# Transformer encoder block on one Trainium2 core: the down projection by seven products of halves

## Chip, core and metric

The kernel runs on one core of one Trainium2 chip. TensorE multiplies matrices, VectorE, ScalarE and GpSimd do the elementwise work, SyncE issues transfers. The metric is the device time of one execution in microseconds (us), lower is better.

## What is computed

One encoder layer over 512 positions and 1024 channels, in float32: two parallel token mixers (multi-scale pooling, and a gated delta rule in both directions), their merge, and a gated feed-forward part. The change concerns the feed-forward part alone:

```python
h2 = rmsnorm(x, norm2_w[l])
u = dwconv_centered(h2 @ ffn_up[l], ffn_conv_w[l], ffn_conv_b[l])   # 1024 -> 2 x 2816, width 3
gate, val = jnp.split(u, 2, axis=-1)
x = x + (jax.nn.silu(gate) * val) @ ffn_down[l]                     # 2816 -> 1024
return rmsnorm(x, final_norm_w)
```

## The kernel before

Every large product runs in float32 quality as three matmuls in a reduced-precision float32 format: each operand is split into a high part (rounded, a ScalarE copy) and a low part (the rest, a subtraction), and `mm3` adds high x high, high x low and low x high into one PSUM bank.

**Order.** The kernel first declares all its work as tasks (`A` for ScalarE, `V` VectorE, `G` GpSimd, `M` TensorE, `L` a transfer issued by SyncE), each with the tiles it reads and writes, an estimated cost and a key. `Planner.run` plays these tasks through with the costs, takes on each engine the ready task with the lowest key, and honours rings of buffers (`RINGS`: name and number of buffers). The instructions are then issued in the order found. Each engine works strictly in that order, so an instruction that waits holds up all that stand behind it on its engine, and a transfer that waits on SyncE holds up all later transfers.

**Up projection.** For each of 22 channel blocks c there are two units, gate and value. A unit loads a weight block of 1024x128 (ring `raw`, 3 buffers), ScalarE casts it to the high part (`whi`, 2 buffers), GpSimd makes the low part in two subtractions of 128x512 (`wlo`, 2 buffers), and TensorE does 24 matmuls with 512 positions as columns into a PSUM bank (`pp`, 3 banks). ScalarE and VectorE turn the bank into the convolution (`conv3`, ring `cv3`, 4 buffers of 128x512). After both units: SiLU on ScalarE, product on VectorE, then the split of the product into high (ScalarE) and low part (VectorE), kept as `a_hl[c]` for the down projection.

**Down projection.** Two halves of the output channels (`hf`). In each, for 22 blocks of 128 rows of `ffn_down` (two per load, split as above by `weights`) and four token tiles of 128 (`t`), three matmuls of 128x128 by 128x512, accumulated over the 22 blocks in four PSUM banks. The last eight blocks of the second half stay in buffers of their own (`wt`), so that the token tiles end one after the other; the last token tile is cut into two column halves. `dadd` adds each bank to the residual `x2[t]`, then `f_part` to `f_out1` do the final normalisation, and two queues write the tile out.

## Time and profile before

| | us |
|---|---|
| median of three runs | 913.95 (913.77 to 915.23) |
| the profiled execution | 914.92 |
| its span, first to last instruction | 913.2 |
| TensorE busy in the span | 901.5 |
| VectorE, ScalarE, GpSimd busy | 428.7, 429.5, 423.9 |
| the up projection in the span | about 545 to 786 |
| the down projection, matmuls | about 786 to 907 |

The profile is one execution. Its rows give for an engine the start, the duration and what the engine waited for before it; busy time by stretch shows which engine fills a stage. Matmuls overlap, so their cost is read from the distance of their starts and not from their duration.

### The profile page before, as it was taken

Reading aid. Unit: us, or ns where it says so; the run is one execution under the profiler, and the core shown is the slowest. Engines: PE = TensorE matmul, PEld = TensorE weight load, DVE = VectorE, ACT = ScalarE, POOL = GpSimd, SP = SyncE. Lnnn points to the kernel's source line nnn. Section 1 sums busy time; section 2 is a strip of 40 time slices with the busy share of each in tenths; the row PEclk is TensorE's granted clock in tenths of the full one; section 3 lists DMA queues with packets and bytes.
Section 4 is the critical chain, followed back from the end, with each engine's and each line's share of the span. In section 5 each row is a group of like instructions: output and inputs, shape, how many; then the busy total and the mean of one; then the engine's idle time right before and its main releaser. Section 6 shows DMA issues by size and latency. Waiting matters only on the chain.

```text
span 913.2 us, 13797 instructions
## 1 busy us (share of the span) xinstructions
PE 901.5 (99%) x5293; PEld 754.2 (83%) x5293; DVE 428.7 (47%) x868; ACT 429.5 (47%) x706; POOL 423.9 (46%) x403
## 2 busy tenths in 40 slices
...
GB/s 201 96 110 104 144 111 202 45 67 66 70 138 130 107 193 25 72 62 112 271 303 242 168 1 93 93 93 99 107 95 93 93 98 108 95 92 93 93 93 93
DMA packets 160983, 104.24 MB, mean 114 GB/s; under 512 B 30566, under 2 KB 141971, under 8 KB 160916
## 3 DMA queue, kind: packets, MB, share of 16 engines
...
q8 instruction: 42, 0.69, 0.3%
q10 hardware_dynamic: 576, 1.05, 0.3%
...
## 4 chain that ended last, share of the span: by engine, by line
PE 94%; DVE 2%; DMA 2%; SPq 1%; ACT 1%; issue 0%; POOL 0%; DVEq 0%; ACTq 0%; POOLq 0%
PE ps_up L372 9%; PE ps_up L373 9%; PE ps_up L371 9%; PE dn L372 4%; PE dn L371 4%; PE dn L373 4%; PE ps_gd L371 2%; PE ps_z L371 2%; PE ps_k L371 2%; PE ps_q L371 2%; PE ps_k L373 2%; PE ps_k L372 2%; PE ps_do L373 2%; PE ps_wo L373 2%; PE ps_wo L371 2%; PE ps_wo L372 2%
## 5 line engine op out<-in xcount | busy, mean ns | idle before, releaser
L399 POOL TENSOR_TENSOR wl_up<-wr_up,wh_up 128x512 fp32r<-128x512 f32 x88 | 111.9, 1292 | 153.9 <-ACT wh_up L395 153.9
L372 PE MATMUL ps_up<-h_lo,wh_up 128*128 128x512 f32 (+1 forms) x368 | 140.0, 381 | 0.3 <-DVE h_lo L545 0.3
L371 PE MATMUL ps_up<-h_hi,wh_up 128*128 128x512 f32 (+1 forms) x368 | 140.1, 381 | 0.0
L373 PE MATMUL ps_up<-h_hi,wl_up 128*128 128x512 f32 (+1 forms) x368 | 139.9, 380 | 0.0
L1615 DVE SCALAR_TENSOR_TENSOR c<-ps_up,fw,c 128x511 f32<-128x511 f32 x88 | 66.1, 751 | 122.4 <-ACT c L1609 116.6
L372 PEld LDWEIGHTS ps_up<-h_lo,wh_up 128*128 128x128 f32 x368 | 69.2, 188 | 13.6 <-DVE h_lo L545 0.5
L373 PEld LDWEIGHTS ps_up<-h_hi,wl_up 128*128 128x128 f32 x368 | 69.2, 188 | 13.2
L371 PEld LDWEIGHTS ps_up<-h_hi,wh_up 128*128 128x128 f32 x368 | 69.2, 188 | 13.0
L399 POOL TENSOR_TENSOR wl_dn<-wr_dn,wh_dn 128x512 fp32r<-128x512 f32 x36 | 46.3, 1306 | 50.0 <-ACT wh_dn L395 50.0
L395 ACT CAST wh_up<-wr_up 128x1024 fp32r<-128x1024 f32 x44 | 46.2, 1051 | 46.7 <-PE ps_up L372 39.4
L372 PE MATMUL dn<-wl_dn,a 128*128 128x512 f32 (+1 forms) x158 | 58.7, 372 | 0.0
L371 PE MATMUL dn<-wh_dn,a 128*128 128x512 f32 (+1 forms) x158 | 58.7, 371 | 0.0
L373 PE MATMUL dn<-wh_dn,a 128*128 128x512 f32 (+1 forms) x158 | 58.6, 371 | 0.0
L1675 DVE TENSOR_TENSOR x<-dn,x 128x512 f32<-128x512 f32 (+1 forms) x9 | 5.7, 633 | 97.6 <-PE dn L373 97.6
L395 ACT CAST wh_dn<-wr_dn 128x1024 fp32r<-128x1024 f32 x18 | 18.9, 1050 | 62.1 <-PE dn L373 60.0
L1637 ACT CAST a<-c 128x512 fp32r<-128x512 f32 x22 | 13.7, 621 | 53.8 <-DVE c L1633 53.8
L399 POOL TENSOR_TENSOR wl_gp<-wr_gp,wh_gp 128x512 fp32r<-128x512 f32 x16 | 21.2, 1348 | 33.8 <-ACT wh_gp L395 33.8
L371 PEld LDWEIGHTS dn<-wh_dn,a 128*128 128x128 f32 x158 | 29.8, 189 | 5.2
L372 PEld LDWEIGHTS dn<-wl_dn,a 128*128 128x128 f32 x158 | 29.8, 189 | 5.2
L373 PEld LDWEIGHTS dn<-wh_dn,a 128*128 128x128 f32 x158 | 29.8, 188 | 5.2
L1609 ACT ACTIVATE c<-ps_up,fw 128x512 f32<-128x512 f32 x44 | 33.9, 770 | 0.0
L399 POOL TENSOR_TENSOR wl_do<-wr_do,wh_do 128x512 fp32r<-128x512 f32 x16 | 24.9, 1581 | 16.3 <-ACT wh_do L395 16.3
...
## 6 DMA issues: line engine op xcount, KB each, us to landing
wr_up<-in_ffn_up_dram SPq DMA_DIRECT2D x44, 512.0 KB, 3.6
wr_dn<-in_ffn_down_dram SPq DMA_DIRECT2D x22, 512.0 KB, 3.5
x<-in_x_dram SPq DMA_DIRECT2D x8, 512.0 KB, 4.8
wr_k<-in_w_in_dram SPq DMA_DIRECT2D x8, 512.0 KB, 5.1
wr_z<-in_w_in_dram SPq DMA_DIRECT2D x8, 512.0 KB, 4.0
wr_q<-in_w_in_dram SPq DMA_DIRECT2D x8, 512.0 KB, 3.7
wr_v<-in_w_in_dram SPq DMA_DIRECT2D x8, 512.0 KB, 3.6
wr_gd<-in_w_in_dram SPq DMA_DIRECT2D x8, 512.0 KB, 3.7
```

Source lines behind the costliest of these rows:

```text
L371: pe.matmul(ps, ahi, bhi, start=first, stop=False)
L372: pe.matmul(ps, ahi, blo, start=False, stop=False)
L373: pe.matmul(ps, alo, bhi, start=False, stop=last)
L395: act.copy(b["hi"], b["raw"])
L399: pool.tensor_tensor(out=b["lo"][:, sl], in0=b["raw"][:, sl], in1=f32(b["hi"][:, sl]), op=ALU.subtract)
L1609: act.activation(b[j], box["ps"], AF.Identity, scale=fw[:, 1, ci : ci + 1], bias=fw[:, 3, ci : ci + 1])
L1615: dve.scalar_tensor_tensor(out=y[:, lo:hi], in0=box["ps"][:, lo + sh : hi + sh], scalar=fw[:, k, ci : ci + 1], in1=y[:, lo:hi], op0=ALU.mu ...
L1637: act.copy(a_hl[c][:, 0, :], b[0])
L1675: dve.tensor_tensor(out=x2[t][:, c0:c1], in0=acc[hf, t, i][:, 0 : c1 - c0], in1=x2[t][:, c0:c1], op=ALU.add)
```

## The change

The down projection, 512 positions by 2816 by 1024, is cut into 2x2x2 halves: 256 positions, 1408 rows (11 blocks, `HK`) and 512 output channels. Instead of eight products of halves, seven are made of sums and differences of halves (`ORDER` is their sequence, `TO` the quarters of the output to which each is added; `dadd` adds one PSUM bank to one to four quarters).

- The left operands (gated products) are no longer split in the up projection as `a_hl`. They are kept in float32 (`a_raw`). For products 1 and 7 the blocks of 256 positions are split during the up projection (`split_part`: ScalarE high, VectorE low; ring `as`, two sets of eleven blocks); for the others during the products before (`left_operand`). The sums and differences (`combine`) are made on VectorE.
- The right operands of products 1, 2 and 3 are halves of `ffn_down`. Those of 5, 6, 7 and 4 are made once, by `t_unit`: for each of 11 row blocks two loads of 512 KB into one buffer (ring `tp`, one buffer), four subtractions in place on GpSimd, four stores of 256 KB to a scratch tensor in DRAM (`t_scr`). These are declared in the up projection with a key behind the other work.
- `down_weights` loads two blocks of 128x512, ScalarE casts each, the low part is made by GpSimd for even blocks and by VectorE for odd ones. There are seven slots for such a split block (`SLOTS`). Of the last product eight blocks stay, as before; its second token tile is cut into two column halves.
- The scratch tile of `f_part` and the output tile `fo` take other rings.

```diff
-        "r4": 4, "nm": 1, "x4": 3, "qe": 4, "ext": 1, "x1": 1, "x2": 1, "xs": 2, "pw": 1, "pwr": 1, "cv3": 4, "fo": 2, "sq2": 1,
+        "r4": 4, "nm": 1, "x4": 3, "qe": 4, "ext": 1, "x1": 1, "x2": 1, "xs": 2, "pw": 1, "pwr": 1, "cv3": 4, "sq2": 1, "as": 2, "tp": 1, "dhl": 3,
     }
-    plan = Planner(RINGS, {"y", "pp", "raw", "whi", "wlo", "f", "z", "q", "v", "r4", "nm", "x4", "qe", "ext", "xs", "pw", "pwr"})
+    plan = Planner(RINGS, {"y", "pp", "raw", "whi", "wlo", "f", "z", "q", "v", "r4", "nm", "x4", "qe", "ext", "xs", "pw", "pwr", "as", "tp", "dhl"})
...
+    t_scr = dram.tile([4, NF // 2, P, 512], F32, name="t_scr")
...
-    a_hl = [None] * NF
+
+
+    HK = NF // 2
+    T_H = (slice(0, 256), slice(256, 512))
+    N_H = (slice(512, 1024), slice(0, 512))
+    ORDER = (1, 7, 5, 6, 3, 2, 4)
+    TO = {1: ((0, 0), (0, 1), (1, 0), (1, 1)), 7: ((1, 0), (1, 1)), 5: ((0, 1), (1, 1)), 6: ((0, 1), (1, 0), (1, 1)),
+          3: ((0, 1),), 2: ((0, 0),), 4: ((1, 0),)}
+    a_raw = [None] * NF
+    sets = {}
+
+    def part_hi(p, i, src):
+        if p not in sets:
+            sets[p] = pools["fp"].tile([P, HK, 2, 256], F32R, tag="as", bufs=RINGS["as"], name=f"as_{p}")
+        act.copy(sets[p][:, i, 0, :], src())
+
+    def part_lo(p, i, src):
+        dve.tensor_tensor(out=sets[p][:, i, 1, :], in0=src(), in1=f32(sets[p][:, i, 0, :]), op=ALU.subtract)
+
+    def split_part(p, i, src, srcn, key):
+
+        A(ca(256), lambda: part_hi(p, i, src), r=[srcn], w=[f"as:{p}#{i}"], key=key)
+        V(cd(256), lambda: part_lo(p, i, src), r=[srcn], w=[f"as:{p}#{i}"], key=key)
+
+    def combine(dst, dstn, x, y, names, op, key):
+        V(cd(256), lambda: dve.tensor_tensor(out=dst(), in0=x(), in1=y(), op=op), r=names, w=[dstn], key=key)
+
+    def blk(c, th):
+        return (lambda: a_raw[c][:, T_H[th]]), f"ar{c}#{th}"
+
+    def t_unit(i, u):
+
+        b = {}
+
+        def load(r):
+            if "w" not in b:
+                b["w"] = pools["fp"].tile([P, 2, D], F32, tag="tp", bufs=RINGS["tp"], name=f"tp_{i}")
+            k = i + HK * r
+            sp.dma_start(b["w"][:, r, :], ffn_down[0][k * P : (k + 1) * P, :])
+
+        w = lambda r, c: b["w"][:, r, N_H[c]]
+        n = lambda r, c: f"tp:{i}#{r}{c}"
+        for r in range(2):
+            L(512, lambda r=r: load(r), r=["pool:fp"], w=[n(r, 0), n(r, 1)], key=u)
+
+        for j, o, x, y in ((0, (0, 0), (0, 1), (0, 0)), (2, (0, 1), (1, 1), (0, 1)), (1, (1, 1), (1, 1), (0, 0)), (3, (1, 0), (1, 0), (1, 1))):
+            G(cp(512), lambda o=o, x=x, y=y: pool.tensor_tensor(out=w(*o), in0=w(*x), in1=w(*y), op=ALU.subtract),
+              r=[n(*x), n(*y)], w=[n(*o)], key=u)
+            L(256, lambda j=j, o=o: sp.dma_start(t_scr[j, i], w(*o)), r=[n(*o)], w=[f"ts{j}#{i}"], key=u)
...
-        def mul(b=b):
-            dve.tensor_tensor(out=b[0], in0=b[0], in1=b[1], op=ALU.mult)
-
-        def hi(c=c, b=b):
-            a_hl[c] = pools["fp"].tile([P, 2, S], F32R, name=f"a_{c}")
-            act.copy(a_hl[c][:, 0, :], b[0])
-
-        def lo(c=c, b=b):
-            dve.tensor_tensor(out=a_hl[c][:, 1, :], in0=b[0], in1=f32(a_hl[c][:, 0, :]), op=ALU.subtract)
+        def mul(c=c, b=b):
+            a_raw[c] = pools["fp"].tile([P, S], F32, name=f"a_{c}")
+            dve.tensor_tensor(out=a_raw[c], in0=b[0], in1=b[1], op=ALU.mult)
 
         A(ca(512), lambda b=b: act.activation(b[0], b[0], AF.Silu), w=[g_], key=u, tab="silu")
-        V(cd(512), mul, r=[v_], w=[g_], key=u)
-        A(ca(512), hi, r=[g_], w=[f"a{c}"], key=u)
-        V(cd(512), lo, r=[g_], w=[f"a{c}"], key=u)
+        V(cd(512), mul, r=[g_, v_], w=[f"ar{c}#0", f"ar{c}#1"], key=u)
+        if c < HK:
+            split_part(1, c, *blk(c, 0), u + 1)
+            s3 = lambda b=b: b[1][:, 0:256]
+            combine(s3, v_, blk(c, 0)[0], blk(c, 1)[0], [f"ar{c}"], ALU.subtract, u + 2)
+            split_part(7, c, s3, v_, u + 3)
+        else:
+            i = c - HK
+            combine(*blk(i, 1), blk(i, 1)[0], blk(c, 1)[0], [f"ar{c}#1"], ALU.add, u + 1)
+            combine(*blk(i, 0), blk(i, 1)[0], blk(i, 0)[0], [f"ar{i}#1"], ALU.subtract, u + 2)
+        if c % 2 == 0:
+            t_unit(c // 2, u + 60)
 
 
     KEEP = 8
-    KS = NF - KEEP
+    KS = HK - KEEP
+    SLOTS = ("whi", "wlo", "dhl", "whi", "wlo", "dhl", "dhl")
     acc = {}
     wt = {}
     dw = {}
 
...
+    def dmm(p, k, j, i):
+        wd = 512 // cut(p, j)
+        if (p, j, i) not in acc:
+            tag = accn(p, j, i)[0]
+            acc[p, j, i] = banks2(f"dn_{p}_{j}")[:, 0, :] if tag == "oo" else bank(tag, f"dn_{p}_{j}")
+        ts_, cs = slice(j * P, (j + 1) * P), slice(i * wd, (i + 1) * wd)
+        w = dw[p, k]["w"]
+        a = sets[p][:, k]
+        mm3(acc[p, j, i][:, 0:wd], a[:, 0, ts_], a[:, 1, ts_], w[:, 0, cs], w[:, 1, cs], k == 0, k == HK - 1)
...
+    def left_operand(p, key):
+
+        for i in range(HK):
+            if p == 3:
+                combine(*blk(i, 0), blk(i + HK, 0)[0], blk(i, 0)[0], [f"ar{i + HK}#0"], ALU.subtract, key + 50 * i)
+            src, n = {5: blk(i, 1), 6: blk(i, 0), 3: blk(i, 0), 2: blk(i + HK, 0), 4: blk(i + HK, 1)}[p]
+            split_part(p, i, src, n, key + 50 * i)
+
+    def right_operand(p, k0, n):
+        if p in (1, 2, 3):
+            r0 = (k0 + (0 if p == 1 else HK)) * P
+            src = ffn_down[0][r0 : r0 + n * P, N_H[1 if p == 3 else 0]]
+            return src.rearrange("(k p) c -> p k c", p=P), []
+        j = {5: 0, 6: 1, 7: 2, 4: 3}[p]
+        return t_scr[j, k0 : k0 + n].rearrange("k p c -> p k c"), [f"ts{j}#{k}" for k in range(k0, k0 + n)]
+
+    turns = {"n": 0}
+
+    def down_weights(p, kk, u):
+
+        n = min(2, HK - 2 * kk)
+        name = f"dn{p}_{kk}"
+        src, deps = right_operand(p, 2 * kk, n)
+        raw = {}
+
+        def load():
+            raw["t"] = wpool.tile([P, n, 512], F32, tag="wraw", bufs=RINGS["raw"], name=f"wr_{name}")
+            sp.dma_start(raw["t"], src)
+
+        L(n * 256, load, r=deps, w=[f"raw:{name}"], key=FEED + u)
+        for j in range(n):
+            k = 2 * kk + j
+            stay = p == 4 and k >= KS
+            b = dw[p, k] = {}
+            if stay:
+                tag, where, b["n"] = None, None, f"kept:{k}"
+            else:
+                tag = SLOTS[turns["n"] % len(SLOTS)]
+                turns["n"] += 1
+                where, b["n"] = ("fp" if tag == "dhl" else None), f"{tag}:{name}{j}"
+
+            def hi(j=j, k=k, b=b, tag=tag, where=where):
+                if tag is None:
+                    b["w"] = wt["h"][(k - KS) // 4].rearrange("p (k a) c -> p k a c", a=2)[:, (k - KS) % 4]
+                else:
+                    b["w"] = (pools[where] if where else wpool).tile(
+                        [P, 2, 512], F32R, tag=tag, bufs=RINGS[tag], name=f"w_{name}{j}"
+                    )
+                act.copy(b["w"][:, 0, :], raw["t"][:, j, :])
+
+            def lo(eng, j=j, b=b):
+                eng.tensor_tensor(out=b["w"][:, 1, :], in0=raw["t"][:, j, :], in1=f32(b["w"][:, 0, :]), op=ALU.subtract)
+
+            A(ca(512), hi, r=[f"raw:{name}"] + (["wth"] if stay else []), w=[b["n"]], key=FEED + u + j)
+            if k % 2:
+                V(cd(512), lambda lo=lo: lo(dve), r=[f"raw:{name}"], w=[b["n"]], key=FEED + u + j)
+            else:
+                G(cp(512), lambda lo=lo: lo(pool), r=[f"raw:{name}"], w=[b["n"]], key=FEED + u + j)
...
+    def done(p, j, i, m):
+
+        e = EVICT + unit["n"] * 100
+        w = 512 // m
+        pn = accn(p, j, i)[1]
+        for th, nh in TO[p]:
+            t, hf = 2 * th + j, 1 - nh
+            c0 = hf * 512 + i * w
+            c1 = c0 + w
+            xn = f"xr{t}#{hf}" if m == 1 else f"xr{t}#{hf}{i}"
+            V(cd(w), lambda t=t, c0=c0, c1=c1: dadd(p, j, i, t, c0, c1), r=[pn] + ([f"xr{t}"] if m > 1 else []), w=[xn], key=FEED + unit["n"] * 100 + 700)
...
+    for p in ORDER:
         u0 = next_unit()
-        unit["n"] += 40
-        for kk in range(NF // 2):
-            stay = hf == 1 and 2 * kk >= KS
...
-
-        def declare(k, t, i, hf=hf, u0=u0, n_=n_):
-            _, whi, wlo = dw[hf, k // 2]
-            M(MM3 / cut(hf, t), lambda: dmm(hf, k, t, i), r=[whi, f"{wlo}#{k % 2}", f"a{k}"],
...
+        unit["n"] += 12
+        if p not in (1, 7):
+            left_operand(p, FEED + u0)
+        for kk in range((HK + 1) // 2):
+            down_weights(p, kk, u0 + 100 * kk)
+
+        def declare(k, j, i, key, p=p):
+            M(MM3 / cut(p, j), lambda: dmm(p, k, j, i), r=[dw[p, k]["n"], f"as:{p}#{k}"], w=[accn(p, j, i)[1]], key=key)
+
+        late = KS if p == 4 else HK
         for k in range(late):
-            for t in range(NT):
-                for i in range(cut(hf, t)):
-                    declare(k, t, i)
-        for t in range(NT):
-            m = cut(hf, t)
-            w = 512 // m
+            for j in range(2):
+                for i in range(cut(p, j)):
+                    declare(k, j, i, u0 + 50 * k + 10 * j + i)
+        for j in range(2):
+            m = cut(p, j)
             for i in range(m):
...
+                for k in range(late, HK):
+                    declare(k, j, i, u0 + 600 + 200 * j + 50 * i + k)
+                done(p, j, i, m)
```

On GpSimd the sums stand between the low parts of the up projection's weights. In the rows, wl is the low part, wr the raw and wh the high part of a unit's weights, named by block and unit. Before:

```order
L399 TENSOR_TENSOR wl_up8_0_6078<-wr_up8_0_5989,wh_up8_0_6077 128x512 x2
L399 TENSOR_TENSOR wl_up8_1_6116<-wr_up8_1_6029,wh_up8_1_6115 128x512 x2
L399 TENSOR_TENSOR wl_up9_0_6155<-wr_up9_0_6066,wh_up9_0_6154 128x512 x2
L399 TENSOR_TENSOR wl_up9_1_6193<-wr_up9_1_6106,wh_up9_1_6192 128x512 x2
L399 TENSOR_TENSOR wl_up10_0_6232<-wr_up10_0_6143,wh_up10_0_6231 128x512 x2
```

After, in the same place, with tp the buffer of a group of weight halves:

```order
L397 TENSOR_TENSOR wl_up8_0_6154<-wr_up8_0_6053,wh_up8_0_6153 128x512 x2
L397 TENSOR_TENSOR wl_up8_1_6196<-wr_up8_1_6110,wh_up8_1_6195 128x512 x2
L1646 TENSOR_TENSOR tp_5_6179<-tp_5_6179 128x512 x3
L397 TENSOR_TENSOR wl_up9_0_6240<-wr_up9_0_6140,wh_up9_0_6239 128x512 x2
L1646 TENSOR_TENSOR tp_5_6179<-tp_5_6179 128x512
L397 TENSOR_TENSOR wl_up9_1_6280<-wr_up9_1_6186,wh_up9_1_6279 128x512 x2
L397 TENSOR_TENSOR wl_up10_0_6329<-wr_up10_0_6225,wh_up10_0_6328 128x512 x2
```

Three subtractions of group 5 now stand ahead of the low part of unit 9_0, and one ahead of that of 9_1.

On SyncE the transfers of the groups stand between the weight loads of the up projection, here the same place. Before:

```order
L387 DMA wr_up9_0_6066<-in_ffn_up_dram 128x8x128
L387 DMA wr_up9_1_6106<-in_ffn_up_dram 128x8x128
L387 DMA wr_up10_0_6143<-in_ffn_up_dram 128x8x128
L387 DMA wr_up10_1_6183<-in_ffn_up_dram 128x8x128
L387 DMA wr_up11_0_6220<-in_ffn_up_dram 128x8x128
```

After:

```order
L388 DMA wr_up9_0_6140<-in_ffn_up_dram 128x8x128
L1648 DMA t_scr_106<-tp_4_6017 128x512
L1638 DMA tp_5_6179<-in_ffn_down_dram 128x1024 x2
L388 DMA wr_up9_1_6186<-in_ffn_up_dram 128x8x128
L388 DMA wr_up10_0_6225<-in_ffn_up_dram 128x8x128
L1648 DMA t_scr_106<-tp_5_6179 128x512 x3
L388 DMA wr_up10_1_6283<-in_ffn_up_dram 128x8x128
L1648 DMA t_scr_106<-tp_5_6179 128x512
L388 DMA wr_up11_0_6312<-in_ffn_up_dram 128x8x128
```

The load of group 5 goes into the buffer that the last store of group 4 reads, and the weight load of unit 9_1 stands behind it.

On VectorE, the down projection before, from its first accumulation (x2 is the residual, dn a PSUM bank, named by half and token tile) to the final normalisation:

```order
L1675 TENSOR_TENSOR x2_0_4716<-dn_0_0_7189,x2_0_4716 128x512
L1675 TENSOR_TENSOR x2_1_4717<-dn_0_1_7198,x2_1_4717 128x512
L1675 TENSOR_TENSOR x2_2_4718<-dn_0_2_7204,x2_2_4718 128x512
L1675 TENSOR_TENSOR x2_3_4719<-dn_0_3_7209,x2_3_4719 128x512
L1704 TENSOR_SCALAR fst_208<-fst_208 128x1
```

After, between products 5 and 6 (as is a set of left blocks, a a gated product, w_dn a weight block by product, pair and place, wr_dn its raw load):

```order
L1617 TENSOR_TENSOR as_6_7629<-a_6_6134,as_6_7629 128x256
L1617 TENSOR_TENSOR as_6_7629<-a_7_6219,as_6_7629 128x256
L1836 TENSOR_TENSOR w_dn6_01_7713<-wr_dn6_0_7664,w_dn6_01_7713 128x512
L1617 TENSOR_TENSOR as_6_7629<-a_8_6307,as_6_7629 128x256
L1617 TENSOR_TENSOR as_6_7629<-a_9_6393,as_6_7629 128x256
L1617 TENSOR_TENSOR as_6_7629<-a_10_6481,as_6_7629 128x256
L1625 TENSOR_TENSOR a_0_5613<-a_11_6567,a_0_5613 128x256
L1836 TENSOR_TENSOR w_dn6_11_7738<-wr_dn6_1_7690,w_dn6_11_7738 128x512
L1625 TENSOR_TENSOR a_1_5703<-a_12_6649,a_1_5703 128x256
```

Where VectorE had four accumulations in the whole first half, it now has left blocks, combinations and every second weight block's low part in one row.

## Rows read from the trace of the kernel before

**Rows 1.** The page's busy time: us (share of the span) and instructions.

```profile
PE 901.5 (99%) x5293; PEld 754.2 (83%) x5293; DVE 428.7 (47%) x868; ACT 429.5 (47%) x706; POOL 423.9 (46%) x403
```

**Rows 2.** Busy time by stage: length; PE, PEld, DVE, ACT, POOL; clock, DMA share, GB/s.

```profile
545.00:786.00 241.00, 240.66 (x1109) 201.19 (x1108) 100.63 (x133) 105.02 (x135) 109.37 (x86) 1.00 0.32 95
786.00:907.00 121.00, 121.00 (x596) 102.55 (x594) 19.12 (x39) 30.58 (x40) 53.75 (x42) 1.00 0.28 96
907.00:913.20 6.20, 0.07 (x1) 0.00 (x0) 1.83 (x6) 0.93 (x2) 0.00 (x0) 0.81 0.23 86
```

**Rows 3.** Matmuls of the down projection, one of three lines: ns min/median/max, starts, forms.

```profile
L371 PE MATMUL dn<-wh_dn,a x158: 277/390/397, 786.1 to 884.4; 128*128 128x512 f32 x130, 128*128 128x256 f32 x28
...
L371 PE MATMUL dn<-wt_hi,a x40: 278/389/397, 884.8 to 906.5; 128*128 128x512 f32 x24, 128*128 128x256 f32 x16
```

**Rows 4.** Timeline of TensorE late in the down projection: start, us, instruction.

```profile
895.04 0.39 PE L371 MATMUL dn<-wt_hi,a 128*128 128x512 f32 x1
...
895.72 0.39 PE L371 MATMUL dn<-wt_hi,a 128*128 128x512 f32 x1
...
901.15 0.28 PE L371 MATMUL dn<-wt_hi,a 128*128 128x256 f32 x1
...
901.51 0.28 PE L371 MATMUL dn<-wt_hi,a 128*128 128x256 f32 x1
```

**Rows 5.** Single lines, elementwise work: ns min/median/max, starts, forms.

```profile
L1637 ACT CAST a<-c x22: 620/621/622, 562.1 to 790.4; 128x512 fp32r<-128x512 f32 x22
...
L1640 DVE TENSOR_TENSOR a<-c,a x22: 691/693/694, 562.8 to 791.0; 128x512 fp32r<-128x512 f32 x22
...
L1706 DVE TENSOR_TENSOR x<-x,nfb x5: 417/680/684, 847.0 to 905.5; 128x512 f32<-128x512 f32 x4, 128x256 f32<-128x256 f32 x1
...
L399 POOL TENSOR_TENSOR wl_dn<-wr_dn,wh_dn x36: 1278/1287/1804, 781.8 to 876.4; 128x512 fp32r<-128x512 f32 x36
```

**Rows 6.** VectorE lines around 460 to 501 us: one with a PSUM operand, two without.

```profile
L1489 DVE TENSOR_TENSOR gdl<-ps_do,gdl x8: 691/692/694, 459.8 to 497.9; 128x512 f32<-128x512 f32 x8
...
L1492 DVE TENSOR_TENSOR m1l<-gdl,m1l x8: 691/693/1653, 460.6 to 498.6; 128x512 f32<-128x512 f32 x8
...
L1499 DVE TENSOR_TENSOR m_lo<-m1l,m_hi x8: 695/1014/1021, 462.0 to 500.9; 128x512 fp32r<-128x512 f32 x8
```

**Rows 7.** Timelines of VectorE and GpSimd over the same stretch of the down projection.

```profile
846.90 0.16 DVE L1705 TENSOR_TENSOR fst<-fst 128x1 f32<-128x1 f32 x1
846.98 0.68 DVE L1706 TENSOR_TENSOR x<-x,nfb 128x512 f32<-128x512 f32 x1
847.58 0.15 DVE L1704 TENSOR_SCALAR fst<-fst 128x1 f32<-128x1 f32 x1
847.76 1.08 DVE L1705 TENSOR_TENSOR fst<-fst 128x1 f32<-128x1 f32 x1
848.76 0.68 DVE L1706 TENSOR_TENSOR x<-x,nfb 128x512 f32<-128x512 f32 x1
...
847.38 3.21 POOL L399 TENSOR_TENSOR wl_dn<-wr_dn,wh_dn 128x512 fp32r<-128x512 f32 x2 [2.91 <-ACT wh_dn L395]
```

**Rows 8.** Timelines of ScalarE and GpSimd in one unit of the up projection.

```profile
633.77 1.05 ACT L395 CAST wh_up<-wr_up 128x1024 fp32r<-128x1024 f32 x1 [1.42 <-PE ps_up L372]
...
639.21 1.05 ACT L395 CAST wh_up<-wr_up 128x1024 fp32r<-128x1024 f32 x1 [0.57 <-PE ps_up L372]
...
634.90 2.54 POOL L399 TENSOR_TENSOR wl_up<-wr_up,wh_up 128x512 fp32r<-128x512 f32 x2 [2.90 <-ACT wh_up L395]
```

**Rows 9.** Transfers by line: KB each, median us from issue to landing.

```profile
wr_up<-in_ffn_up_dram SPq DMA_DIRECT2D x44, 512.0 KB, 3.6
...
z_scr<-zo SPq DMA_DIRECT2D x8, 256.0 KB, 2.0
```

**Rows 10.** Chain of waits from 438 to 454 us: start, us, what.

```profile
440.07 4.87 DMA m_scr<-gpl
...
445.36 6.54 DMA wr_do<-in_dn_out_dram
```

More of the change, by code (lines that the diff above doesn't have):

```diff
@@ L379, in next_unit, with weights @@
         return unit["n"] * 100.0
-    def weights(src, kt, n, name, u, keep=None, room=()):
+    def weights(src, kt, n, name, u):
         b = {}
@@ L389, in hi @@
         def hi():
[L390 to L394 removed]
+            b["hi"] = wpool.tile([P, kt, n], F32R, tag="whi", bufs=RINGS["whi"], name=f"wh_{name}")
+            b["lo"] = wpool.tile([P, kt, n], F32R, tag="wlo", bufs=RINGS["wlo"], name=f"wl_{name}")
             act.copy(b["hi"], b["raw"])
```

101 lines of the change are left out of this document (33 added, 68 removed).

## The prediction

> **What bounds the kernel now.** I read the page's busy table first, then the busy time by stage, then the order of the instructions. TensorE is busy 901.5 of 913.2 us [rows 1], and in the two stages that the change touches it has no gaps: 240.66 of 241 us in the up projection (545 to 786 us) and 121.0 of 121 us in the down projection (786 to 907), both at a granted clock of 1.00, the 2.4 GHz level [rows 2]. The other three engines stand idle for more than half of either stage. So a matmul that is taken out is worth its full pitch, unless what replaces it makes TensorE wait. The profiled execution took 914.92 us, 1.72 around its span, and lies 0.97 above the median of the three runs (913.95); the sum is made against 914.92 and then moved down by 0.97.
>
> **Term 1, matmuls removed: -15.4 us.** Before, the down projection issues 130 + 24 = 154 matmuls of 512 columns and 28 + 16 = 44 of 256 on each of three lines [rows 3]: 462 and 132. After: seven products, 11 row blocks, two token tiles, three matmuls each, 462 in all; the second tile of the last product is cut in two, so 429 of 512 columns and 66 of 256 (the order of the changed program has these counts). Three matmuls of 512 columns start 0.68 us apart (895.04 to 895.72), so 0.2275 each; three of 256 take 0.36 (901.15 to 901.51), so 0.12 [rows 4]. Before: 462 x 0.2275 + 132 x 0.12 = 120.9, which is the stage's 121.0. After: 429 x 0.2275 + 66 x 0.12 = 105.5. The difference is 15.4. One product is 66 x 0.2275 = 15.0 us. The end after the last matmul (6.2 us [rows 2]) has the same instructions, two tiles instead of one to write from: nothing.
>
> **Term 2, the weights of the products.** 77 tiles of 128x512 are split into high and low part instead of 44, one per 6 x 0.2275 = 1.365 us. Per product ScalarE casts eleven at 0.62 [rows 5] and eleven left blocks of 256 columns at about 0.41 (by the step from 0.62 at 512 columns to 1.05 at 1024 [rows 5, 8]): 11.3 of 15.0 us, fits. The low parts of even blocks go to GpSimd, six at 1.29 = 7.7 us; those of odd blocks to VectorE, five at 0.69 = 3.5 [rows 5]. Transfers: 77 x 256 KB in 105 us is 191 GB/s against 96 at a DMA share of 0.28 [rows 2], so about 0.56: fits. Seven slots for split tiles give a lead: a slot comes free six tiles (8.2 us) ahead of its turn, cast and subtraction take 2.0, so weights may be 6 us late before TensorE notices.
>
> **Term 3, VectorE and GpSimd in the down projection: 0 to +14 us, I take +5.** VectorE, nearly idle there before (19.12 of 121 us), gets per product eleven left low parts of 256 columns (0.42, the shortest of L1706 [rows 5]) = 4.6, five weight low parts = 3.5, and four accumulations (28 over the seven products) at 0.69 (the line with a PSUM operand, [rows 6]) = 2.8: 10.9 of 15.0 us by itself. But these do not run beside GpSimd freely. An addition of two SBUF operands took 0.69 us alone and 1.01 to 1.65 beside GpSimd, while one with a PSUM operand kept 0.69 [rows 6]. One pair of rows shows how: a one-column addition that takes 0.16 takes 1.08 when it starts 0.38 us into a GpSimd subtraction: it ends when that one's 1.29 and its own 0.16 are over (848.83 against 848.84). The GpSimd pair, 2.54 elsewhere [rows 8], stretches to 3.21, and the next VectorE product, at 848.76, went ahead of its waiting second half [rows 7]. So the two take turns, instruction by instruction. Then their times add: over the five products in which left blocks are made (7, 5, 6, 3, 2; 75.1 us of TensorE) GpSimd has 30 x 1.29 = 38.7; VectorE 25 x 0.69 + 55 x 0.42 = 40.4, the eleven combinations for product 3 4.6, and four final-norm products 3.4. That is 87.1 in 75.1 us, 12 too many, 6 of which the lead of the weight slots swallows; for accumulations from PSUM that meet no GpSimd instruction I allow 2 on top. Upper end: 14. Lower end: independent VectorE instructions start about 0.08 before the one ahead ends (847.58 against 846.98 + 0.68 [rows 7]); 95 of them give back 7.6, and the rest is inside the lead: 0. A gain is excluded, TensorE has nothing left to skip. I take 5, nearer to the lower end, since the left blocks have a whole product's time of lead, but not at it: the load of a pair of weights waits until the low parts three pairs ahead are made, and of its 6.8 us (five tiles) cast, subtraction and a landing of 3.6 [rows 9] take 5.0, so a VectorE that is over 2 us late delays the casts too. This order is what the third pair of order rows shows: runs of two-operand subtractions on VectorE, with a weight's low part every third or fourth row, for which TensorE waits if it is late.
>
> The Trainium skill (SBUF — State Buffer, "Who interferes with whom") states that such a pair shares one port under a lock that is held for the whole instruction, and that the other engine fully blocks. The trace agrees (1.08 against 0.16). By that rule the sum has the term just worked out; if the two only slowed each other in part, both would fit into 75 us and the term would be 0.
>
> **Term 4, the sums of weight halves in the up projection: 0 to +5 us, I take +1.** Eleven groups of two loads of 512 KB, four GpSimd subtractions and four stores of 256 KB. GpSimd: 109.4 us [rows 2] + 44 x 1.29 = 166 of 241. The order puts the groups into the first 33 of 44 projection units, one per three or four units. In such a stretch of three (16.3 us) GpSimd has ten instructions, 12.9 us, and VectorE's two-operand work, per pair of units one product at 0.69 and three of 256 columns at 0.42, adds 1.95 x 1.5 = 2.9: 15.8 of 16.3. Full, but the pair of low parts of a unit now ends at 637.44 when its turn comes at about 639.1, the first half about 3 us ahead [rows 8], and three subtractions in a row (3.9) overrun GpSimd's idle time of 2.90 [rows 8] by 1.0, plus at most 1.9 of VectorE turns: 2.9, just inside those 3 us. Transfers double to 191 GB/s at a share of about 0.60. What is queued behind: on GpSimd the next unit's low part, on SP the next units' loads, behind each store that waits for a subtraction and each group load that waits until the last store of the group before has landed. A weight load can go some 12 us before its cast (three raw slots at 5.44 us a unit, less the 3.7 of cast and subtractions [rows 8]) and lands in 3.6 [rows 9], so SP may stand some 8 us. VectorE's and ScalarE's new rows of 256 columns are covered: 100.6 and 105 of 241 us busy [rows 2], with about 20 and 5 more. The left blocks replace one cast of 512 columns by two of 256 in eleven units and drop it in the other eleven.
>
> **Sum:** 914.92 - 15.4 + 5 + 1 = 905.5 on the profiled execution, 904.5 for the median.
>
> **Rivals.** *All hidden* (898 to 901.5): the turns cost no more than the 6 us lead. For it: the overlap of starts above, and GpSimd's time that falls beside VectorE's accumulations. Against it: 87 us of turns in 75. *The shared turns are the bound* (907.5 to 912.5): VectorE never idles from product 7 on and each low part is late by up to 14 us in sum. For it: [rows 6], where an addition lost up to 0.96 us. VectorE's own work in those five products, 24 accumulations with it, is 65 us of the 81 that 75 and the lead give, so it decides when each of the 30 GpSimd instructions costs VectorE over 0.54 us. *Slower than before, by the one buffer of the group loads* (about 918): the next group's load stands at the head of SP until the last store lands. The trace has that chain once: a store landed in 4.87 us and the weight load behind it in 6.54 [rows 10], 11.4 us, where the order leaves 8.3 to 9.6 us between a group's last subtraction and the next group's first. If every one of ten rounds went so, GpSimd would start 2 to 3 us late with 1 to 3 us of other delay on top, past the 3 us of slack by about 2: 20 us, 898.5 + 20 = 918.5. Against it: such a store has a median of 2.0 and a load of 3.6 [rows 9], 5.6 in all. It decides from a sum of about 10 us. *The clock falls* (about 914): it was 0.81 in the last 6.2 us, where TensorE stood [rows 2]; if waits in the down projection let a third of its 105 us run at 1.2 GHz, that third costs 17 us less what the waits themselves then need no more, about 15. Against it: a tile is never more than a few us late. That the change saves no matmuls is excluded by the order.
>
> **How the numbers follow.** Forecast (waits of 3 to 9 us, 901.5 to 907.5) 0.45; all hidden 0.25; turns as the bound 0.18; slower by the group buffer 0.07; clock 0.05. A measurement of this kernel tells about 0.2% from no change, that is 1.8 us: faster is below 912.1. Faster: 0.45 + 0.25 + most of 0.18 = 0.86; same: the rest and most of the clock case, 0.07; slower 0.07. The range 898 to 912 leaves out the last two cases and the last tenth or so of the third, 0.14.
>
> **What would show it.** Right: 495 dn matmuls at 0.2275 and 0.12; the up stage within 1 to 2 us of 241; in products 6, 3 and 2 TensorE waiting for a low part, by VectorE more than by GpSimd; VectorE's 256-column subtractions well above 0.42 in the mean; GpSimd's above 1.29. Wrong: TensorE idle at a unit of the up projection behind GpSimd or a weight load; waits for ScalarE or for a transfer in the down projection; a granted clock under 1.00 there; no waits at all, which would be the first rival.

## The result, and the profile after

The changed kernel takes 905.3 us in the median of eight executions (903.13 to 910.9), the kernel before 913.86 (eight, 912.87 to 916.71): a ratio of 0.9906, 95% interval 0.9883 to 0.9929. The prediction was 904.5, range 898 to 912. The profiled execution took 903.13, 2.2 under that median; its span is 901.4.

The page's busy times, which answer to [rows 1]:

```profile
PE 887.2 (98%) x5194; PEld 739.5 (82%) x5194; DVE 543.9 (60%) x1022; ACT 461.9 (51%) x816; POOL 491.4 (55%) x445
```

Busy time by stage, with the columns of [rows 2]:

```profile
545.00:786.00 241.00, 240.66 (x1108) 201.12 (x1107) 133.85 (x167) 101.32 (x140) 171.74 (x130) 1.00 0.58 192
786.00:901.00 115.00, 107.15 (x496) 87.79 (x494) 102.68 (x165) 67.68 (x148) 58.73 (x40) 1.00 0.55 176
```

TensorE lost 99 matmuls (5293 to 5194). The up projection, from its first matmul to the first of the down projection, takes 241.63 us in both profiles, although GpSimd does 62 us more in it and the transfers have doubled. In the down projection VectorE went from 19 to 103 us.

TensorE's timeline in that stage: the first matmul of the down projection, then the first and the last longer gap. The last column is idle time and what ended it.

```profile
785.84 0.39 PE L372 MATMUL dn<-w_dn,as 128*128 128x512 f32 x1
...
877.17 0.39 PE L372 MATMUL dn<-w_dn,as 128*128 128x512 f32 x1
878.50 0.50 PE L373 MATMUL dn<-w_dn,as 128*128 128x512 f32 x1 [0.93 <-DVE fst L1751]
...
887.56 0.50 PE L373 MATMUL dn<-wt_lo,as 128*128 128x512 f32 x1 [1.07 <-POOL wt_lo L1836]
```

The seven products start at 785.84, 800.80, 815.76, 830.72, 845.68, 860.64 and 875.78: five are exactly 14.96 us long and the sixth 15.14. The last matmul starts at 895.48. I took from each start the one before it and its pitch (0.2275 or 0.12): what is left over 0.06 us adds up to 4.4 us, called the gaps below. Of this 4.3 lie in the last product, product 4. (The idle time in the rows adds up to 2.6 only: a matmul's row reaches past the pitch, and the first two matmuls after a wait start 0.33 us apart and not 0.23.)

Instructions of VectorE and GpSimd in the down projection, by line and form: busy us, mean ns, idle time before.

```profile
L1836 POOL TENSOR_TENSOR w_dn<-wr_dn,w_dn 128x512 fp32r<-128x512 f32 x36 | 52.8, 1470 | 42.7 <-ACT w_dn L1833 40.2 <-DVE x L1722 2.4
L1617 DVE TENSOR_TENSOR as<-a,as 128x256 fp32r<-128x256 f32 x55 | 33.9, 668 | 0.0
L1836 DVE TENSOR_TENSOR w_dn<-wr_dn,w_dn 128x512 fp32r<-128x512 f32 x30 | 30.8, 1028 | 6.6 <-ACT w_dn L1833 6.6
L1722 DVE TENSOR_TENSOR x<-dn,x 128x512 f32<-128x512 f32 x27 | 17.4, 678 | 0.0
```

The subtractions of two SBUF operands take 0.67 us for 256 columns and 1.03 for 512, where [rows 5] has 0.42 and 0.69. The accumulations with a PSUM operand stay at 0.68.

How late is a low part? Its first reader is the second matmul of its block (L373), in block k of a product at the product's start + k x 1.365 + 0.23 us. Four low parts by VectorE on its timeline, of products 7, 3, 2 and 4:

```profile
806.23 1.13 DVE L1836 TENSOR_TENSOR w_dn<-wr_dn,w_dn 128x512 fp32r<-128x512 f32 x1
...
848.90 1.78 DVE L1836 TENSOR_TENSOR w_dn<-wr_dn,w_dn 128x512 fp32r<-128x512 f32 x1
...
864.21 0.68 DVE L1836 TENSOR_TENSOR w_dn<-wr_dn,w_dn 128x512 fp32r<-128x512 f32 x1
...
876.66 1.78 DVE L1836 TENSOR_TENSOR w_dn<-wr_dn,w_dn 128x512 fp32r<-128x512 f32 x1
```

The first ends at 807.36, 5.95 us before its reader is due (block 9: 800.80 + 12.29 + 0.23 = 813.31). The second, block 5, has 2.05 left, the third, block 3, ends at 864.89 with 0.07 left, and the fourth is 1.07 late. The mean over the five low parts of each product, worked out in the same way:

```
product          1     7     5     6     3     2     4
lead left, us   5.1   5.1   6.1   4.5   2.9   0.9   first block 1.07 late
```

So the lead melted by 1.5 to 2 us a product in 6, 3 and 2, and TensorE noticed in the one after.

### The profile page after: what moved, and what is told of

It is laid out like the page before. It is cut to its first block, busy times and chain, and to the rows that moved or that the text cites. A ratio compares the mean times of both kernels' runs of the same rounds, so it can differ in the third digit from the quotient of the medians.

```text
span 901.4 us, 14200 instructions
## 1 busy us (share of the span) xinstructions
PE 887.2 (98%) x5194; PEld 739.5 (82%) x5194; DVE 543.9 (60%) x1022; ACT 461.9 (51%) x816; POOL 491.4 (55%) x445
## 4 chain that ended last, share of the span: by engine, by line
PE 85%; DVE 9%; DMA 2%; issue 2%; SPq 1%; ACT 1%; POOL 1%; POOLq 0%; DVEq 0%; ACTq 0%
PE ps_up L373 9%; PE ps_up L374 9%; PE ps_up L372 9%; DVE as L1617 3%; DVE w_dn L1836 2%; PE ps_z L372 2%; PE ps_k L372 2%; PE ps_gd L372 2%; PE ps_q L372 2%; PE ps_k L374 2%; PE ps_k L373 2%; PE ps_wo L372 2%; PE ps_wo L374 2%; PE ps_wo L373 2%; PE ps_q L374 2%
## 5 line engine op out<-in xcount | busy, mean ns | idle before, releaser
L373 PE MATMUL ps_up<-h_lo,wh_up 128*128 128x512 f32 (+1 forms) x368 | 139.9, 380 | 0.3 <-DVE h_lo L543 0.3
L1646 POOL TENSOR_TENSOR tp<-tp 128x512 f32<-128x512 f32 x44 | 61.5, 1398 | 37.3 <-DMA tp<-in_ffn_down_dram 33.7
L373 PEld LDWEIGHTS ps_up<-h_lo,wh_up 128*128 128x128 f32 x368 | 69.2, 188 | 13.7 <-DVE h_lo L543 0.5
L1836 POOL TENSOR_TENSOR w_dn<-wr_dn,w_dn 128x512 fp32r<-128x512 f32 x38 | 55.8, 1472 | 43.5 <-ACT w_dn L1833 41.0
L1833 ACT CAST w_dn<-wr_dn 128x512 fp32r<-128x512 f32 x69 | 41.1, 620 | 34.4 <-DMA wr_dn<-in_ffn_down_dram 10.9
L373 PE MATMUL dn<-w_dn,as 128*128 128x512 f32 x141 | 54.4, 386 | 0.9 <-DVE fst L1751 0.9
L374 PE MATMUL dn<-w_dn,as 128*128 128x512 f32 x141 | 54.2, 385 | 0.0
L372 PE MATMUL dn<-w_dn,as 128*128 128x512 f32 x141 | 54.2, 384 | 0.0
L1617 DVE TENSOR_TENSOR as<-a,as 128x256 fp32r<-128x256 f32 x66 | 42.8, 692 | 0.0
L1614 ACT CAST as<-a 128x256 fp32r<-128x256 f32 x66 | 24.0, 403 | 30.4 <-DVE a L1680 27.8
L1836 DVE TENSOR_TENSOR w_dn<-wr_dn,w_dn 128x512 fp32r<-128x512 f32 x31 | 32.2, 1037 | 7.1 <-ACT w_dn L1833 7.1
L397 POOL TENSOR_TENSOR wl_k<-wr_k,wh_k 128x512 fp32r<-128x512 f32 x16 | 20.2, 1284 | 26.7 <-ACT wh_k L393 22.4
L397 POOL TENSOR_TENSOR wl_v<-wr_v,wh_v 128x512 fp32r<-128x512 f32 x16 | 20.4, 1294 | 24.4 <-ACT wh_v L393 24.4
```

What stands on the lines that cost most here:

```text
L372: pe.matmul(ps, ahi, bhi, start=first, stop=False)
L373: pe.matmul(ps, ahi, blo, start=False, stop=False)
L374: pe.matmul(ps, alo, bhi, start=False, stop=last)
L397: pool.tensor_tensor(out=b["lo"][:, sl], in0=b["raw"][:, sl], in1=f32(b["hi"][:, sl]), op=ALU.subtract)
L1614: act.copy(sets[p][:, i, 0, :], src())
L1617: dve.tensor_tensor(out=sets[p][:, i, 1, :], in0=src(), in1=f32(sets[p][:, i, 0, :]), op=ALU.subtract)
```

## The experiments

Times are medians, the ratio is to the kernel before on the same chip. Theory A is that of the prediction, the turns of VectorE and GpSimd. Rivals came up with the place of the waits: GpSimd's own lateness (A2), the loads of the last product (B), and VectorE's sheer load.

**GpSimd's weight subtractions left out.** The output lacks the low parts of even row blocks.

```
-mm3(..., w[:, 0, cs], w[:, 1, cs], ...)
+mm3(..., w[:, 0, cs], w[:, k % 2, cs], ...)
-                G(cp(512), lambda lo=lo: lo(pool), ...)
+                pass
```

> The kernel after, without the 38 weight subtractions of GpSimd in the down projection: for even row blocks TensorE reads the high part where the low part would be, so the low part of these blocks is left out. Matmuls, casts and loads are the same in number. After has 4.4 us of TensorE waits in the down projection, all of them in the last product. Theory A (turns of VectorE and GpSimd make VectorE late, VectorE's lateness delays loads and casts): VectorE's 256-column subtractions fall from a mean of 0.69 us to 0.42, the 512-column ones from 1.04 to 0.69, and the waits go: 901 us (900 to 902). Theory B (the last product takes its kept weight blocks every 0.68 us instead of every 1.365, because its two token tiles are finished one after the other, and three raw slots with landings of 3.6 us cannot feed that): VectorE's durations fall in the same way, but 1.5 to 3 us of waits stay in the last product, for casts that wait for a load: 902.5 to 904.

898.75 us (898.09 to 899.73), ratio 0.983 (0.9814 to 0.9847); no gap in the 495 matmuls. Groups of the same stage, as above:

```profile
L1617 DVE TENSOR_TENSOR as<-a,as 128x256 fp32r<-128x256 f32 x55 | 20.1, 420 | 1.0 <-ACT as L1614 1.0
L1836 DVE TENSOR_TENSOR w_dn<-wr_dn,w_dn 128x512 fp32r<-128x512 f32 x29 | 20.1, 692 | 21.6 <-ACT w_dn L1833 21.6
```

VectorE's durations are back at 0.42 and 0.69, and it now waits for casts where it ran without a pause before. That is 2 us more gain than I expected of A, and B as it stands is out: the loads and the kept blocks are the same, and no matmul waits. (In after GpSimd makes 42 low parts of these weights, not 38.) GpSimd no longer holds a raw slot here either; the next run keeps that.

**GpSimd's subtractions kept, but read by nobody.** The same low parts are missing from the output.

```
+    def spare(src, high):
+        pool.tensor_tensor(out=idle["t"], in0=src, in1=f32(high), op=ALU.subtract)
...
-                G(cp(512), lambda lo=lo: lo(pool), ...)
+                G(cp(512), lambda ...: spare(raw["t"][:, j, :], b["w"][:, 0, :]), ...)
```

> As the run without GpSimd's weight subtractions, but GpSimd does each of them all the same, into a spare tile that nobody reads; TensorE reads the high part in place of these low parts, which are left out of the result. So the port is used as in after, and nobody waits for GpSimd itself, but the raw slots are still held until it has read them. Theory A: VectorE's 256-column subtractions stay at a mean near 0.69 us and 3 to 4.4 us of waits stay: 904 to 905.5. Rival A2 (TensorE waits because GpSimd's own low parts come late, with the turns of no consequence for VectorE's part): waits fall to 1 or less, 901 to 902. Theory B: the raw slots are as late as in after, waits for casts behind loads stay, waits for GpSimd's low parts (about 1.3 of the 4.4) go: 903.5 to 904.5.

904.38 us (903.11 to 906.86), ratio 0.9894 (0.9873 to 0.9916); gaps of 5.1 us. The same groups of that run:

```profile
L1842 DVE TENSOR_TENSOR w_dn<-wr_dn,w_dn 128x512 fp32r<-128x512 f32 x30 | 32.9, 1096 | 8.8 <-ACT w_dn L1839 8.7
L1617 DVE TENSOR_TENSOR as<-a,as 128x256 fp32r<-128x256 f32 x55 | 29.3, 584 | 0.0
```

VectorE is slow again. The three longest gaps of TensorE (1.10, 1.14 and 1.14 us) all end with a VectorE low part, and none can be for GpSimd's result, which has no reader. These three low parts took 1.77, 1.78 and 1.61 us where 0.69 is normal: the stretch of that one instruction is as long as the gap, or nearly (0.92 of the last 1.14).

```profile
864.42 1.77 DVE L1842 TENSOR_TENSOR w_dn<-wr_dn,w_dn 128x512 fp32r<-128x512 f32 x1
...
877.96 1.78 DVE L1842 TENSOR_TENSOR w_dn<-wr_dn,w_dn 128x512 fp32r<-128x512 f32 x1
...
887.76 1.61 DVE L1842 TENSOR_TENSOR wt_lo<-wr_dn,wt_lo 128x512 fp32r<-128x512 f32 x1
```

5.6 us between these two runs are what GpSimd's instructions cost by being there. A2 is out. Besides the turns, these instructions still hold raw slots until they have read them, but little hangs on that: the load queue (SyncE) waited 7.9 us for them and 73.4 for VectorE's low parts.

**All low parts on VectorE**, the computation complete.

```
-            if k % 2:
+            if True:
                 V(cd(512), lambda lo=lo: lo(dve), ...)
```

> After with all 77 low parts of weights in the down projection on VectorE, none on GpSimd; the computation is complete. VectorE's work per product becomes 11 x 0.42 + 11 x 0.69 + 4 x 0.69 = 15.0 us of a product's 15.0, less about 0.08 for each start before the end of the one ahead (2.0 us). Theory A: with no turns VectorE does about 13 of 15 us per product, the waits go down to 0 to 2 us: 901 to 903, faster than after. A rival by load (VectorE is simply full, the turns cost less than the extra work): waits grow to 6 to 10 us: 907 to 911. Theory B: durations as for A, but 2 to 4 us of waits stay in the last product, where VectorE has low parts every 0.68 us and the raw slots are as few as before: 903 to 905.

910.24 us (908.88 to 912.34), ratio 0.9957 (0.9943 to 0.9971): 5 us slower than after, which looks like the rival by load. It isn't: only 3.1 us are gaps in TensorE. The last matmul starts at 893.78 and the span ends at 907.5, 13.7 us later, where after has 5.9. VectorE's timeline shows why:

```profile
887.27 0.68 DVE L1753 TENSOR_TENSOR x<-x,nfb 128x512 f32<-128x512 f32 x1
892.67 0.69 DVE L1722 TENSOR_TENSOR x<-dn,x 128x512 f32<-128x512 f32 x1 [4.72 <-PE dn L374]
893.28 0.14 DVE L1751 TENSOR_SCALAR fst<-fst 128x1 f32<-128x1 f32 x1
```

From 887.9 it stood 4.7 us at an accumulation that waited for TensorE, with three final-norm products and three sums of squares behind it in its order, while ScalarE, which goes on from these sums, stood from 885.7 to 897.0. The planner had taken VectorE for slower than it is (0.77 us for 512 columns against a measured pitch of 0.60) and put them there. So the run tells nothing of the load; the run with corrected costs, below, does.

**The last product's weights loaded early**, into activation tiles that are free, in place of the three raw slots.

```
+            sp.dma_start(a_raw[2 * kk + j], t_scr[3, 2 * kk + j])
...
-                act.copy(b["w"][:, 0, :], raw["t"][:, j, :])
+                act.copy(b["w"][:, 0, :], a_raw[k] if p == 4 else raw["t"][:, j, :])
```

> After, with one edit: the eleven weight blocks of the last product are loaded one by one into the eleven tiles of activations that are no longer needed once the third-last-but-one left operand is made, instead of through the three raw slots of two blocks. The computation is complete; GpSimd and VectorE have the same subtractions as in after. Theory B (the raw slots cannot feed the last product's kept blocks, one every 0.68 us): loads run ahead, casts no longer stand behind a landing, the 4.4 us of waits fall to 0 to 1.5: 900.5 to 902.5. Theory A (turns alone): VectorE's and GpSimd's instructions of the last two products still collide and are as many, the waits stay at 3 to 4.5 us: 904 to 905.5.

910.66 us (907.96 to 913.82), ratio 0.995 (0.9932 to 0.9968): worse than either theory said. The gaps are 10.8 us and none lies in the last product; the longest, 6.1, is in product 3. Of the 10.8, 2.7 are not waits but matmuls at half pace behind that gap, at a granted clock of 0.50 (the 1.2 GHz level). The profiled execution, 913.82, is the slowest of the five, and 4.1 us of what it has over after lie ahead of the down projection. The planner did the last product's subtractions where they met those of products 3 and 2. VectorE, then GpSimd, over the same ten microseconds:

```profile
858.57 1.51 DVE L1617 TENSOR_TENSOR as<-a,as 128x256 fp32r<-128x256 f32 x1
860.00 1.51 DVE L1617 TENSOR_TENSOR as<-a,as 128x256 fp32r<-128x256 f32 x1
861.43 1.51 DVE L1617 TENSOR_TENSOR as<-a,as 128x256 fp32r<-128x256 f32 x1
...
867.08 1.74 DVE L1845 TENSOR_TENSOR w_dn<-wr_dn,w_dn 128x512 fp32r<-128x512 f32 x1
...
858.38 1.41 POOL L1845 TENSOR_TENSOR wt_hi<-a,wt_hi 128x512 fp32r<-128x512 f32 x1 [2.15 <-ACT wt_hi L1842]
859.76 1.47 POOL L1845 TENSOR_TENSOR w_dn<-wr_dn,w_dn 128x512 fp32r<-128x512 f32 x1
861.19 1.48 POOL L1845 TENSOR_TENSOR wt_hi<-a,wt_hi 128x512 fp32r<-128x512 f32 x1
```

Each VectorE instruction of 256 columns waits for exactly one of GpSimd's, for six in a row, and the weight's low part for which TensorE stands comes behind them, at 867.08. This is the plainest picture of the turns, and it shows that the waits go where the work of the two meets, not where the weights are needed fastest.

**All low parts on VectorE, the planner's costs corrected.** The first edit of the run that kept the computation complete, and:

```
 def cd(n):
-    return 0.18 + n * 0.00115
+    return 0.06 + n * 0.00106 if DOWN[0] else 0.18 + n * 0.00115
```

(DOWN[0] is 1 while the down projection is declared.)

> As the run with all 77 low parts on VectorE, with one more edit: in the down projection the planner's cost of a VectorE instruction is set to the pitch that the traces show, 0.60 us for 512 columns and 0.33 for 256, in place of 0.77 and 0.47. The same instructions, only their order changes: the four products with the final norm's weights stand before the last low parts instead of behind the last accumulation. That run lost 3.1 us in waits and 13.7 us lay behind its last matmul where after has about 6. Theory A (without GpSimd's instructions VectorE has about 73 us of work for the 75 of products 7 to 2, and what was lost there was lost by order): waits of 0 to 2 us, an end of 6: 898.5 to 901, faster than after by 4 to 7 us. Rival (VectorE is too full with all low parts, whatever the order): still 906 to 910.

899.59 us (898.5 to 900.69), ratio 0.9843 (0.9829 to 0.9858); no gaps in the down projection, and 6 us from the last matmul's start to the end of the span.

```profile
L1839 DVE TENSOR_TENSOR w_dn<-wr_dn,w_dn 128x512 fp32r<-128x512 f32 x65 | 43.2, 684 | 5.9 <-ACT w_dn L1836 5.5
L1620 DVE TENSOR_TENSOR as<-a,as 128x256 fp32r<-128x256 f32 x55 | 20.8, 416 | 0.0
```

One engine does twice the low parts and has them in time, since each costs what it costs alone. The rival by load is out. With the early loads added:

> The two edits together: all low parts on VectorE with the planner's costs at 0.60 and 0.33 us, and the last product's eleven weight blocks loaded early, into tiles of activations that are no longer needed. With after's split of the work the early loads lost 10.8 us in waits, 6.1 of them at one block of the fifth product, behind eight left low parts on VectorE that took 9.26 us beside GpSimd. Theory A: without GpSimd the same eight take about 3 us, and nothing waits: 898.5 to 900.5, the same as with the costs alone within 1 us. Rival (the early loads themselves are at fault, by filling ScalarE and VectorE with work that is not due yet): 4 us or more slower than with the costs alone, 903 to 907.

898.94 us (898.58 to 899.54), ratio 0.9836 (0.982 to 0.9853), no gaps: early loads do no harm where GpSimd is quiet.

**All low parts on GpSimd**, the other way (`if False:` in the place of `if k % 2:`).

> After with all 77 low parts of weights in the down projection on GpSimd, none on VectorE; the computation is complete. GpSimd then has 11 x 1.29 = 14.2 us per product of 15.0. If the two engines take turns, VectorE's eleven left low parts of 0.42 add to it, 18.8 us per product and more with the eleven combinations: 4 us late per product over five products, less 6 of lead, 15 us or so behind: 914 to 922. If they do not exclude one another, GpSimd fits by itself and VectorE has less to do than in after: 900 to 904.

917.46 us (915.2 to 918.48), ratio 1.0034 (1.002 to 1.0047); 13.2 us of gaps, near the 15 that the turns gave; some 2 of them are matmuls at a granted clock of 0.50, behind a gap of 4.3. VectorE, with less to do than in after, is slower for each instruction:

```profile
L1836 POOL TENSOR_TENSOR w_dn<-wr_dn,w_dn 128x512 fp32r<-128x512 f32 x66 | 92.6, 1434 | 9.4 <-ACT w_dn L1833 9.0 <-PE dn L374 0.3
L1617 DVE TENSOR_TENSOR as<-a,as 128x256 fp32r<-128x256 f32 x55 | 61.5, 1184 | 0.0
```

**The sums of weight halves alone**: the kernel before with `t_unit` called as in after, and nobody reading its stores.

```
+        if c % 2 == 0:
+            t_unit(c // 2, u + 60)
```

> The kernel before, with the sums of weight halves made and stored in the up projection as in after, and read by nobody. This is the fourth term by itself, taken as +1 in the prediction. By the trace of after (up projection 241.6 us long in both kernels) it costs 0 to 0.7 us: 914 to 915. By the rival of the one buffer of the group loads it would be 10 us or more: 924 and above.

914.25 us (913.44 to 915.74), ratio 0.9999 (0.999 to 1.0009): nothing.

**The corrected costs alone**, the low parts shared as in after:

> After with its split of the low parts between VectorE and GpSimd unchanged, and the planner's costs of VectorE in the down projection set to 0.60 and 0.33 us: the second edit of the run with all low parts on VectorE, without the first. Theory A (GpSimd's instructions hold VectorE up, whatever the order): the costs of 0.60 and 0.33 are not true beside GpSimd, 3 to 6 us of waits stay, 903.5 to 907. Rival (the order was what after lost its time by, and the port cost nothing that a good order does not cover): waits under 1 us, 898.5 to 901, as with the two edits together.

902.97 us (901.58 to 905.9), ratio 0.9884 (0.9861 to 0.9907), half a microsecond under the range of A; gaps of 4.3 us. TensorE's waits in the down projection (us in total, times, longest):

```profile
PE dn L376 <- DVE wt_lo L1839: 2.5, 2, 1.5
PE dn L376 <- POOL w_dn L1839: 0.6, 1, 0.6
PE dn L376 <- DVE wt_hi L1839: 0.2, 1, 0.2
```

The order alone doesn't remove the waits. Whether it is worth something took three more runs side by side:

> The kernel after once more, on the same chip as the next two runs, to set beside them: 904 to 906.5.

> The kernel after with the planner's costs of VectorE at 0.60 and 0.33 us, once more, beside after itself: whether the new order alone is worth anything. If the port sets the waits, it is within 1.5 us of after, 903.5 to 906; if the order does, 899 to 902.

> All low parts on VectorE with the planner's costs at 0.60 and 0.33 us, beside after on the same chip: 898.5 to 900.5, 5 to 7 us faster than after, if the port is what after loses its time by.

After: 906.01 (903.02 to 910.48), 0.9912 (0.9889 to 0.9934), gaps 3.8. New order, shared: 903.86 (902.23 to 907.16), 0.9881 (0.9861 to 0.9901), gaps 5.7, of which 1.5 are matmuls at the lower clock (below). New order, VectorE alone: 898.2 (897.52 to 900.17), 0.982 (0.9801 to 0.9839), no gaps. Taking the low parts off GpSimd is worth 5.7 us under the same planner's costs, as the second and third differ by it. That GpSimd is also the slower engine for a low part (1.29 against 0.69 us) is in this number, but not in the 5.6 of the unread subtractions. The order alone gave 2.3 us (against the first runs of after) and 2.2 in the medians, but its intervals overlap with after's and its profiles show no smaller waits (4.3 and 4.2 against 4.4 and 3.8): open. The last of the three beats both kernels, by 7.8 us and 16.5.

## Why the prediction was right, and where not

**Term 1, the matmuls: right.** Without gaps (all low parts on VectorE, costs corrected) the stage runs from 785.69 to 890.75 + 0.12, 105.2 us, against 105.5 reckoned.

**Term 2, the weights of the products: right in every rate.** Casts took 0.62 and 0.40 us, the DMA share was 0.55, the clock 1.00. One sentence was wrong: "one per 6 x 0.2275 = 1.365 us" does not hold for the last product. There the first token tile is finished before the second over eight kept blocks, so that a block is due every 0.68 us. I had read the order and not asked at what pace it takes the weights. Of the 4.3 us in that product 3.1 come at these blocks, from 881.17 on, where two casts stand behind a raw slot's load (ScalarE's timeline); 1.2 came before them, at its second block.

```profile
882.16 0.62 ACT L1833 CAST wt_hi<-wr_dn 128x512 fp32r<-128x512 f32 x1 [3.46 <-DMA wr_dn<-t_scr]
882.68 0.61 ACT L1833 CAST wt_lo<-wr_dn 128x512 fp32r<-128x512 f32 x1
885.31 1.14 ACT L1833 CAST wt_lo<-wr_dn 128x512 fp32r<-128x512 f32 x2 [2.01 <-DMA wr_dn<-t_scr]
```

The slots are only the carrier, by the coupling that the term named: the load of a pair goes when the low parts of the pair three before it are made. SyncE's waits in the down projection show for whom the loads stood (us in total, times, longest):

```profile
SPq L1812 <- DVE w_dn L1836: 73.8, 29, 5.1
SPq L1812 <- POOL w_dn L1836: 6.4, 6, 1.8
```

The chain behind the longest gap has the same link, from a VectorE low part over the load and the cast to GpSimd's:

```profile
881.06 0.61 DVE wt_hi L1836
...
881.73 3.56 DMA wr_dn<-t_scr
...
885.31 0.63 ACT wt_lo L1833
...
886.01 0.82 POOL wt_lo L1836
```

With all low parts on VectorE the same three slots feed the same pace with no gap.

**Term 3, the turns: right in mechanism and size (4.4 and 3.8 us of gaps, taken as 5), wrong in place.** That GpSimd's instructions are the cause, and not their results, is shown by the two runs that differ in its unread subtractions alone; that they act through the turns, by the stretched low parts at which TensorE's gaps end there. The step that failed is the step from the sum to the place: "in products 6, 3 and 2 TensorE waiting". The lead did melt in exactly these, from 6.1 to 0.9 us, and they lived on it; the product after them paid. And the waits by name were 0.9 for VectorE and 1.3 for GpSimd, not the other way round, though the chain above leads from the longest one for GpSimd back to VectorE. ScalarE's 0.2, for a cast behind a load, is a sign that the prediction had set for being wrong.

The term's upper end doesn't follow from its own numbers: 12 too many, less 6 of lead, with 2 on top is 8; the 14 left the lead out. The sum of turns was also too large: it said 12 us too many over the five products from 7 to 2, and the lead fell by 4.2 (5.1 in product 1, 0.9 in product 2). A turn is cheaper than the sum of two durations: in the early-loads run a GpSimd and a VectorE instruction together take 1.43 us (860.00 to 861.43), not 1.29 + 0.42 = 1.71. Of these 0.28 us, 0.08 are the early start of VectorE's next instruction, which the lower end had counted; the other 0.20 I had not. Thirty GpSimd instructions at 0.28 are 8.4 us, if each meets such a subtraction, which would leave 4 of the 12. The value taken, 5, was chosen between the two ends and not worked out; that the gaps came to 4.4 with a sum of turns that was too large is in part luck.

The Trainium skill (SBUF — State Buffer, "SBUF: two separate sides") has the pair locked for a whole instruction, the other engine fully blocked. The alternation one by one agrees; the 1.43 us for two instructions of 1.29 and 0.42 do not add up to one lock after the other at the profile's durations; why, no run here shows.

**Term 4, the sums: taken as +1, in the profiles 0 to 1.7.** Added to the kernel before they gave a ratio of 0.9999, and the first profile of after shows nothing of them. But in seven of the twelve profiled executions with after's up projection TensorE waits once, at 590 to 594 us, for a low part that stands behind three sums on GpSimd, and the up projection takes 242.2 to 243.4 us instead of 241.63. In the second profile of after:

```profile
590.83 0.50 PE L374 MATMUL ps_up<-h_hi,wl_up 128*128 128x512 f32 x1 [0.23 <-POOL wl_up L397]
```

In the run with all low parts on VectorE and corrected costs, where the stage took 242.87 us, the chain of that wait begins with a load of weight halves that was late for GpSimd:

```profile
573.65 6.31 DMA tp<-in_ffn_down_dram
```

This is another of the prediction's signs of being wrong ("TensorE idle at a unit of the up projection behind GpSimd"), at a price inside the term's range; the mean over the twelve is 0.7 us. Transfers of after (KB, median us to landing):

```profile
wr_up<-in_ffn_up_dram SPq DMA_DIRECT2D x44, 512.0 KB, 3.9
tp<-in_ffn_down_dram SPq DMA_DIRECT2D x22, 512.0 KB, 5.1
t_scr<-tp SPq DMA_DIRECT2D x44, 256.0 KB, 3.1
```

Store and next load, 3.1 + 5.1 = 8.2 us, stay under the 10 from which the rival of the group buffer decides. GpSimd's subtractions there had a median of 1.30 us.

**The rivals.** "All hidden" is what happens without GpSimd's instructions: its price, 898 to 901.5, is that of four runs here. "Turns as the bound" is nearest to the run with all low parts on GpSimd, at 917.46. "The clock falls" did not happen in the two profiles of after, where the clock stayed at 1.00 to the last matmul. But it fell to 0.50, the 1.2 GHz level, in three other runs: within the gap of 6.1 us of the early loads, within one of 4.3 with all low parts on GpSimd, and behind two waits of 0.8 and 1.3 us in the second run of the new order, shared, whose row is

```profile
889.50:892.60 3.10, 3.10 (x13) 2.73 (x12) 2.27 (x5) 0.75 (x2) 0.00 (x0) 0.50 0.70 267
```

It cost 2.7, some 2 and 1.5 us there. So "a tile is never more than a few us late" was no ground to rule it out; the price of 15 was far too high for waits of this size.

**The sum.** For the profiled execution it gave 905.5 and 903.13 was measured, for the median 904.5 and 905.3. The prediction moved the median down by 0.97 from the profiled execution, as in the kernel before; in after it lies 2.2 above. That the median came out within 0.8 is in part luck.

**What stays open.** Since the median of after lies 2.2 us above its profiled execution, others lose more than 4.4 us; where, no trace shows: the two that were profiled, both the fastest of their series, have 4.4 and 3.8 us of gaps. The wait near 591 us and the lower clock, both seen in other runs, are candidates. In each of the four runs without GpSimd's low parts and without gaps the executions lie within 1.0 to 2.7 us, those of after within 7.8 and 7.5, so the missing time seems to go with GpSimd too; that is not shown.
